# Where the sample's mixer-input splits stand in the ScalarE and DVE queues of a two-request encoder kernel

## The chip, the core and the metric

The kernel runs on one core of one Trainium2 chip. A core has five engines, each with a queue of its own: TensorE (PE, matmuls; PEld are its weight loads), VectorE (DVE), ScalarE (ACT), GpSimd (POOL) and SyncE (SP), which here only issues DMAs. ACT issues the weight loads beside its own work. The metric is the device time of one launch in microseconds (us); lower is better. The time before is 2271.11 us, the median of 3 runs (2269.18 to 2272.93).

## What is computed

One encoder layer is applied to two requests with shared weights: the prompt (1024 positions) and the sample (512 positions), each with 16 learned meta positions in front. Cut to what matters:

```python
n = rms_norm(h)
qa, ka, va, qb, kb, vb = split(n @ w_in)
A = softmax(rope(qa) @ rope(ka).T / 8) @ va          # 8 heads of 64, keys shared by 4
B = (softmax(q0 @ k0.T) - lam * softmax(q1 @ k1.T)) @ vb   # 4 heads, two maps each
h = h + concat(A, B) @ w_out                          # the mixer's output
h = h + conv_glu(rms_norm(h))                         # gate with a width-3 convolution, d_ff 2816
y = rms_norm(h)
```

All of it is float32. To keep that precision on TensorE every matmul operand x is split into two parts, hi = round(x) in the type fp32r and lo = x - hi, and a product is taken as hi*hi + hi*lo + lo*hi.

## The kernel before

Tiles hold features on the 128 partitions and positions along the free axis. The stages follow in the order: projection of the sample, attention of the sample merged with the projection of the prompt, then attention of the prompt (s = 0) merged with the sample's mixer output and ConvGLU (the generator `sample()`), then the prompt's own mixer output and ConvGLU. The change lies at the start of the third of these.

**The merge.** `merge` (L755) takes turns between two generators. With `LEAD2 = 60000` the prompt's attention is written first, for two whole blocks and one softmax of the third; then the sample's work begins. On PE the first four steps of the sample's work are held behind the second block's last matmul (`HOLD`). An attention block is one head with 512 queries: four softmaxes (`softmax`, L394) and one product with the values (`weighted_v`, L411). A softmax is six score matmuls into the one wide PSUM tile `ps_s` (L401, L402), a scaled minimum on DVE that reads it and so frees it (L405), and an exponential on ACT (L408). `weighted_v` transposes the probabilities 128 keys at a time into one of two PSUM tiles `ps_t` (L422), splits them (`split`: the cast `pt_hi` on ACT, L123, and the subtraction `pt_lo` on DVE, L124) and multiplies (L436, L437). The last 32 keys are split into one tile, `pt_hi[0:32]` by ACT and `pt_hi[32:64]` by DVE (L442), and multiplied at L446. `reciprocals` (L450) writes a row of reciprocals to DRAM through a copy on ACT (L457).

**The sample's mixer output.** `mixer_out` (L584) loads the sample's attention output from DRAM into `h` by eight DMAs on SP (L612), one for each 128 features; then come 16 splits, eight feature tiles by two chunks of 258 and 256 positions (L616): the cast `xhi<-h` on ACT and the subtraction `xlo<-h,xhi` on DVE. Then for each of eight tiles of outputs and each chunk come 24 matmuls (`dense`, L134, lines L129 to L131). The residual `res` is loaded by SP (L622), and where the chunk is one position short its last column is set to zero by a small DVE memset (L625).

**What sets the order.** The program goes through a scheduler that simulates a timeline, picks per engine what is ready in that timeline, and fixes one order of instructions for each engine. On the chip every engine goes through its own list in that order; an instruction that waits for a semaphore holds up all that stands behind it on its engine. `tc.issue_after(x)` adds an order: what is traced inside it on the engine of x stands behind x. Memory is taken from pools; a tile that takes the place of an older one waits until the older one's readers are done, DMAs among them. DMAs count on eight semaphores, DMAHW0 to DMAHW7, in turn, and a DMA first waits for the one before it on the same semaphore.

Of the kernel before, what the change touches and what calls it, by code (L numbers as in the profile page):

```python
# [12 lines left out]
F32 = mybir.dt.float32  # L13
F32R = mybir.dt.float32r
AF = mybir.ActivationFunctionType
ALU = mybir.AluOpType
# [6 lines left out]
KT = D // P  # L23
# [39 lines left out]
def token_chunks(s):  # L63


    ends = [c + w + 2 for c, w in even_chunks(SEQS[s], 510)]
    return [(a, b - a) for a, b in zip([0] + ends, ends)]
# [36 lines left out]
def pool(ctx, g, name, bufs, side):  # L104
    return ctx.enter_context(g.tc.tile_pool(name=name, bufs=bufs, side=side, reuse_waits="tile"))
# [14 lines left out]
def split(g, hi, lo, src, lo_engine=None):  # L120

    nc = g.nc
    nc.scalar.copy(hi, src)  # L123
    (lo_engine or nc.vector).tensor_tensor(out=lo, in0=src, in1=hi.bitcast(F32), op=ALU.subtract)  # L124


def mm3(g, ps, whi, wlo, xhi, xlo, start, stop):
# [6 lines left out]
def dense(g, ps, w, xhi, xlo, c0, cw, order=range(KT)):  # L134

    whi, wlo = w
    for i, k in enumerate(order):
        g.mark = mm3(g, ps, whi[:, k * P:(k + 1) * P], wlo[:, k * P:(k + 1) * P],
                     xhi[k][:, c0:c0 + cw], xlo[k][:, c0:c0 + cw], i == 0, i == KT - 1)


def load_weight(g, src, lo_engine=None, hi_engine=None):

    nc = g.nc
    w = g.wp.tile([P, D], F32, name="w_f", tag="w_f", bufs=NRAW)
    nc.scalar.dma_start(out=w, in_=src)
    hi = g.wp.tile([P, D], F32R, name="w_hi", tag="w_hi")
    lo = g.wp.tile([P, D], F32R, name="w_lo", tag="w_lo")
    if hi_engine:
        hi_engine.tensor_copy(hi, w)  # L150
        nc.vector.tensor_tensor(out=lo, in0=w, in1=hi.bitcast(F32), op=ALU.subtract)
    else:
        split(g, hi, lo, w, lo_engine)
    return hi, lo
# [194 lines left out]
def attention(ctx, g, s, side):  # L349
    nc, tc = g.nc, g.tc  # L350
# [14 lines left out]
    op = pool(ctx, g, f"ao{s}", 2, side)  # L365
# [14 lines left out]
    def load_k(j, m):  # L380
        k = kp.tile([P, ne], F32R, name="k", tag="k")
        stacked(k[:, :n], j, m, 0, 0, n)
        if ne > n:
            stacked(k[:, n:], j, m, 0, 0, ne - n)
        return k
# [25 lines left out]
    def weighted_v(pl, v, diff):  # L411

        W = sum(p.shape[0] for p in pl)
        o = g.psum.tile(P, W, "o")
        v, v_tail = v

        def transposed(k0, kw):
            tps = g.psum.tile(kw, W, "t")
            c = 0
            for p in pl:  # L420
                M = p.shape[0]
                nc.tensor.transpose(tps[:, c:c + M], p[:, k0:k0 + kw], g.ident[:M, :M])  # L422
                c += M
            return tps

        for i in range(nf):
            tps = transposed(i * P, P)
            hi = ptp.tile([P, 512], F32R, name="pt_hi", tag="pt_hi")[:, :W]
            lo = ptp.tile([P, 512], F32R, name="pt_lo", tag="pt_lo")[:, :W]
            split(g, hi, lo, tps)  # L430
            if diff:
                nc.tensor.matmul(o, lhsT=v[:, i, 0:P], rhs=hi, start=i == 0, stop=False)  # L432
                nc.tensor.matmul(o, lhsT=v[:, i, P:2 * P], rhs=hi, start=False, stop=False)
                nc.tensor.matmul(o, lhsT=v[:, i, 0:P], rhs=lo, start=False, stop=False)
            else:
                nc.tensor.matmul(o, lhsT=v[:, i, :], rhs=hi, start=i == 0, stop=False)  # L436
                nc.tensor.matmul(o, lhsT=v[:, i, :], rhs=lo, start=False, stop=False)  # L437
            yield 5 * W

        tps = transposed(n - 32, 32)  # L440
        parts = ptp.tile([P, 512], F32R, name="pt_hi", tag="pt_hi")[:, :W]
        split(g, parts[0:32], parts[32:64], tps)  # L442
        if diff:
            nc.scalar.copy(parts[64:96], tps)
        rows = v_tail.shape[0]
        g.mark = nc.tensor.matmul(o, lhsT=v_tail, rhs=parts[:rows], start=False, stop=True).ins  # L446
        yield 2 * W
        return o, W
# [36 lines left out]
    for kv in range(2):  # L485
        k = load_k(KA, kv)
        v = load_v(0, P, kv * P)
        for i in range(4):
            h = kv * 4 + i
            for b in range(nblk):  # L490
                q = load_q(QA + 2 * kv, i, NMETA + 512 * b, 512)
                load_r()
                pl = []
                l = sp.tile([P, 4], F32, name="l_a", tag="l_a", bufs=3)
                for t in range(4):
                    pl.append(softmax([x[:, t * P:(t + 1) * P] for x in q], k, l[:, t:t + 1]))
                    yield 2 * n
                cols = slice(1 + 512 * b, 513 + 512 * b)
                reciprocals(l, g.rT[s][h, cols].rearrange("(t p) -> t p", p=P))
                o, W = yield from weighted_v(pl, v, False)  # L500
                oa = finish_a(o, W)
                store_a()
                late.append((oa, g.rT[s][h:h + 1, cols], g.oT[s][h * HD:(h + 1) * HD, cols]))
# [12 lines left out]
        for i in range(4):  # L516
            h = kv * 4 + i
# [34 lines left out]
    for h in range(4):  # L552
# [3 lines left out]
        for blk in blocks:  # L556
            c0 = blk[0][0]
# [8 lines left out]
def add_square(g, tp, acc, h, j, c0, cw, eng, bufs=2):  # L566

    nc = g.nc
    hs = h[:, j, c0:c0 + cw]
    if j == 0:  # L570
        nc.scalar.activation(acc, hs, AF.Square)
    else:
        sq = tp.tile([P, cw], F32, name="sq", tag="sq", bufs=bufs)
        nc.scalar.activation(sq, hs, AF.Square)
        eng.tensor_tensor(out=acc, in0=acc, in1=sq, op=ALU.add)


def mean_rsqrt(g, tp, out, acc, cw, tag="mm"):
    ps = g.psum.tile(P, cw, tag)
    g.nc.tensor.matmul(ps, lhsT=g.ones_d, rhs=acc, start=True, stop=True)  # L580
    rsqrt_newton(g, tp, out, ps, cw)


def mixer_out(g, s, st, side, whole, tag):  # L584

    nc, tc = g.nc, g.tc
    C = SEQS[s] + 2
    h, rstd = st.h, st.rstd
    chunks = token_chunks(s)
    cm = max(w for _, w in chunks)  # L590
    with ExitStack() as es:
        mp = pool(es, g, f"fm{s}", 3, side)
        waiting = []

        def finish():
            while waiting:
                c0, cw, acc = waiting.pop(0)
                mean_rsqrt(g, mp, rstd[:, c0:c0 + cw], acc, cw, tag)

        for group in ([chunks] if whole else [[c] for c in chunks]):  # L600
            if whole:
                (xhi, xlo), base = [[x[:, k] for k in range(KT)] for x in st.x], 0
            else:
                xhi = [mp.tile([P, cm], F32R, name="xhi", tag=f"xhi{k}", bufs=2) for k in range(KT)]
                xlo = [mp.tile([P, cm], F32R, name="xlo", tag=f"xlo{k}", bufs=2) for k in range(KT)]
                base = group[0][0]
            acc = mp.tile([P, sum(w for _, w in group)], F32, name="acc", tag="acc", bufs=1 if whole else 2)
            if group[0][0] == 0:

                nc.vector.memset(h[:, :, C - 1:], 0.0)  # L610
                for k in range(KT):
                    nc.sync.dma_start(out=h[:, k, :C - 1], in_=g.oT[s][k * P:(k + 1) * P])  # L612
            for k in range(KT):
                for c0, cw in group:
                    b = c0 - base
                    split(g, xhi[k][:, b:b + cw], xlo[k][:, b:b + cw], h[:, k, c0:c0 + cw])  # L616
            for j in range(KT):
                w = load_weight(g, g.w_out[j])
                for c0, cw in group:
                    real = min(cw, C - 1 - c0)  # L620
                    res = mp.tile([P, cm], F32, name="res", tag="res", bufs=4)[:, :cw]
                    nc.sync.dma_start(out=res[:, :real],  # L622
                                      in_=g.xT[s][j * P:(j + 1) * P, NMETA - 1 + c0:NMETA - 1 + c0 + real])
                    if real < cw:
                        nc.vector.memset(res[:, real:], 0.0)  # L625
                    ps = g.psum.tile(P, cw, tag)
                    dense(g, ps, w, xhi, xlo, c0 - base, cw)
                    nc.vector.tensor_tensor(out=h[:, j, c0:c0 + cw], in0=ps, in1=res, op=ALU.add)
                    add_square(g, mp, acc[:, c0 - base:c0 - base + cw], h, j, c0, cw, nc.gpsimd, 1)
                    yield 24 * cw  # L630
                if j == ML:
                    finish()
            waiting += [(c0, cw, acc[:, c0 - base:c0 - base + cw]) for c0, cw in group]
        finish()
# [326 lines left out]
```

## Time and profile before

| | |
|---|---|
| median of 3 runs | 2271.11 us |
| the profiled execution | 2271.76 us |
| its span in the profile | 2270.0 us |
| mean granted TensorE clock | 0.967 |
| PE busy | 2139.6 us (94%) |
| DVE busy | 1272.2 us (56%) |
| ACT busy | 1039.8 us (46%) |
| POOL busy | 669.2 us (29%) |

The profile's times count from the start of its span. A row of the timeline gives start, duration, engine, line of the code, operation, the tile written and the tiles read, shapes, and in brackets how long the engine was idle before the row and what ended that. Rows of SP (SPq) are DMA issues, not the transfers. Tile names in the profile leave the buffer numbers out; in the order of the built program they are kept, so that blocks can be told apart: `pt_hi_6134` to `pt_hi_6222` belong to the prompt's first attention block, `pt_hi_6294` to `pt_hi_6382` to its second, and `p_6399`, `p_6490`, `p_6501`, `p_6512` are the softmaxes of the third; `p_6777` to `p_6842` those of the fourth.

### The profile page before, as it was taken

To read this page: it belongs to the slowest core of one execution; us is meant where nothing else is said; L and a number is where in the kernel's file an instruction comes from. 1 tells how busy PE (TensorE), PEld (TensorE's weight loads), DVE (VectorE), ACT (ScalarE), POOL (GpSimd) and SP (SyncE) were. 2 spreads that over 40 slices of the span, in tenths; PEclk is the share of its full clock that TensorE was granted. 3 is DMA by queue.
4 is the path that set the end of the run, shared out by engine and by line. 5 is a ranking of instruction groups with operands and counts; after the bars stand their busy time and mean duration, and the time that the engine had idled before them with its cause. 6 is when DMAs were issued, how large, how long until landed. Compare 5 with 4: busy or idle time off the path is not lost.

```text
span 2270.0 us, 32333 instructions
## 1 busy us (share of the span) xinstructions
PE 2139.6 (94%) x12442; PEld 1919.7 (85%) x12442; DVE 1272.2 (56%) x2203; ACT 1039.8 (46%) x1830; POOL 669.2 (29%) x514
## 2 busy tenths in 40 slices
PE   7887999986699999999999997999999999999997
PEld 6886999985598888888999996988888888888887
DVE  6635554454558667667777775774433444433446
ACT  5434554656547445466777775542122221122224
POOL 5862345531023212234444443431111001111005
PEclk8998999996899999999999998999999999999999
DMA  6573454443332232233323224631111111111112
GB/s 204 178 221 112 142 162 129 155 157 105 106 102 82 74 101 81 72 94 92 118 94 107 88 69 151 197 99 49 40 47 56 47 47 47 45 40 56 47 38 75
DMA packets 114259, 222.76 MB, mean 98 GB/s; under 512 B 16312, under 2 KB 67384, under 8 KB 113592
## 3 DMA queue, kind: packets, MB, share of 16 engines
q1 hardware_dynamic: 85304, 115.82, 16.0%
q10 hardware_dynamic: 28800, 104.87, 14.8%
q8 instruction: 98, 1.61, 0.3%
q14 instruction: 57, 0.47, 0.1%
HBM read 172.10 MB, written 48.55 MB: 97 GB/s over the span
## 4 chain that ended last, share of the span: by engine, by line
PE 81%; DMA 6%; DVE 5%; ACT 3%; issue 2%; POOL 1%; SPq 1%; DVEq 0%; ACTq 0%; POOLq 0%
PE ps_mm L129 20%; PE ps_mm L130 20%; PE ps_mm L131 20%; PE ps_t L422 5%; PE ps_s L401 3%; PE ps_s L402 3%; PE ps_o L437 2%; PE ps_o L436 1%; DMA q<-qk 1%; DMA v<-v 1%; PE ps_p L129 1%; PE ps_p L131 1%; PE ps_p L130 1%; PE ps_o L432 1%; DMA w_f<-w_out 1%
## 5 line engine op out<-in xcount | busy, mean ns | idle before, releaser
L129 PE MATMUL ps_mm<-xhi,w_hi 128*128 128x512 f32 (+6 forms) x1968 | 666.3, 339 | 0.7 <-ACT xhi L123 0.4
L130 PE MATMUL ps_mm<-xlo,w_hi 128*128 128x512 f32 (+6 forms) x1968 | 659.6, 335 | 0.6 <-POOL xlo L124 0.6
L131 PE MATMUL ps_mm<-xhi,w_lo 128*128 128x512 f32 (+6 forms) x1968 | 658.1, 334 | 0.0
L129 PEld LDWEIGHTS ps_mm<-xhi,w_hi 128*128 128x128 f32 x1968 | 373.7, 190 | 28.1 <-issue 1.7
L130 PEld LDWEIGHTS ps_mm<-xlo,w_hi 128*128 128x128 f32 x1968 | 373.8, 190 | 26.2 <-POOL xlo L124 1.3
L131 PEld LDWEIGHTS ps_mm<-xhi,w_lo 128*128 128x128 f32 x1968 | 373.3, 190 | 25.0 <-issue 0.5
L123 ACT CAST w_hi<-w_f 128x1024 fp32r<-128x1024 f32 x134 | 139.3, 1048 | 402.7 <-PE ps_mm L130 364.2
L405 DVE TENSOR_SCALAR_CACHE_REDUCE p<-ps_s 114x1044 f32<-114x1044 f32 (+5 forms) x212 | 223.4, 1054 | 127.7 <-PE ps_s L402 107.1
L124 POOL TENSOR_TENSOR a_lo<-gate,a_hi 128x512 fp32r<-128x512 f32 x66 | 99.4, 1507 | 660.3 <-ACT a_hi L123 659.3
L123 ACT CAST pt_hi<-ps_t 128x512 fp32r<-128x512 f32 (+6 forms) x360 | 168.9, 482 | 200.3 <-PE ps_t L422 169.7
L703 DVE TENSOR_TENSOR h<-ps_mm,h 128x512 f32<-128x512 f32 (+1 forms) x288 | 182.0, 644 | 121.8 <-PE ps_mm L131 121.1
L408 ACT ACTIVATE p<-p,nm 114x1040 f32<-114x1040 f32 (+5 forms) x212 | 215.2, 1015 | 74.0 <-DVE p L405 73.0
L124 DVE TENSOR_TENSOR pt_lo<-ps_t,pt_hi 128x512 fp32r<-128x512 f32 (+4 forms) x312 | 171.7, 564 | 125.5 <-ACT pt_hi L123 123.7
L130 PE MATMUL ps_mm<-a_lo,w_hi 128*128 128x512 f32 (+1 forms) x576 | 216.1, 378 | 0.0
L131 PE MATMUL ps_mm<-a_hi,w_lo 128*128 128x512 f32 (+1 forms) x576 | 216.1, 378 | 0.0
L129 PE MATMUL ps_mm<-a_hi,w_hi 128*128 128x512 f32 (+1 forms) x576 | 214.8, 385 | 0.4 <-DVE h L703 0.4
L401 PE MATMUL ps_s<-k,q 128*114 128x348 f32 (+4 forms) x552 | 180.8, 333 | 30.8 <-DMA q<-qk 16.9
L422 PE MATMUL ps_t<-ident,p 128*128 128x128 f32 (+7 forms) x1188 | 184.2, 270 | 2.4 <-ACT r_rows L457 2.0
L402 PE MATMUL ps_s<-k,q 128*114 128x348 f32 (+4 forms) x552 | 175.2, 323 | 4.4 <-DMA q<-qk 4.4
L124 DVE TENSOR_TENSOR w_lo<-w_f,w_hi 128x1024 fp32r<-128x1024 f32 x100 | 124.1, 1250 | 82.8 <-ACT w_hi L123 82.7
L422 PEld LDWEIGHTS ps_t<-ident,p 128*128 128x128 f32 (+7 forms) x1188 | 142.9, 136 | 31.7 <-issue 4.0
L532 POOL TENSOR_TENSOR p<-p 114x1040 f32<-114x1040 f32 (+2 forms) x56 | 115.0, 2053 | 128.9 <-ACT p L531 127.0
(189 smaller groups left out, 3547.2 us busy)
## 6 DMA issues: line engine op xcount, KB each, us to landing
w_f<-w_gate ACTq DMA_DIRECT2D x44, 512.0 KB
w_f<-w_up ACTq DMA_DIRECT2D x44, 512.0 KB
w_f<-w_down ACTq DMA_DIRECT2D x44, 512.0 KB
w_f<-w_in ACTq DMA_DIRECT2D x36, 512.0 KB
w_f<-w_out ACTq DMA_DIRECT2D x32, 512.0 KB
q<-qk SPq DMA_DIRECT2D x48, 256.0 KB
q<-qk SPq DMA_DIRECT2D x48, 171.0 KB
qk<-hi SPq DMA_DIRECT2D x20, 384.0 KB
```

The costliest lines, as they stand in the source:

```text
L123: nc.scalar.copy(hi, src)
L124: (lo_engine or nc.vector).tensor_tensor(out=lo, in0=src, in1=hi.bitcast(F32), op=ALU.subtract)
L129: nc.tensor.matmul(ps, lhsT=whi, rhs=xhi, start=start, stop=False)
L130: nc.tensor.matmul(ps, lhsT=whi, rhs=xlo, start=False, stop=False)
L131: return nc.tensor.matmul(ps, lhsT=wlo, rhs=xhi, start=False, stop=stop).ins
L401: nc.tensor.matmul(ps[:, i], lhsT=q[0], rhs=kc, start=True, stop=False)
L402: nc.tensor.matmul(ps[:, i], lhsT=q[1], rhs=kc, start=False, stop=True)
L405: nc.vector.tensor_scalar(out=p.rearrange("p (i w) -> p i w", i=nch), in0=ps, scalar1=-HD ** -0.5, scalar2=3.0e38, op0=ALU.mult, op1=ALU.m ...
L408: nc.scalar.activation(p, p, AF.Exp, bias=nm, scale=-1.0, accum_out=l)
L422: nc.tensor.transpose(tps[:, c:c + M], p[:, k0:k0 + kw], g.ident[:M, :M])
L532: nc.gpsimd.tensor_tensor(out=p0, in0=p0, in1=p1, op=ALU.add)
L703: nc.vector.tensor_tensor(out=hs, in0=ps, in1=hs, op=ALU.add)
```

## The change

`split` returns its two instructions, `weighted_v` keeps those of the last split of its block in `g.marks`, and `mixer_out` for the sample (`whole`) traces its 16 splits inside `issue_after` of both. When `mixer_out` is traced, the marks are those of the prompt's second attention block. So the casts stand behind `pt_hi_6382` on ACT and the subtractions behind `pt_hi_6382` on DVE. No instruction is added or taken away. From the first moved instruction on the scheduler orders anew; the lists of all engines differ up to about PE instruction 7900 of 12323 and are the same behind it.

```diff
 def split(g, hi, lo, src, lo_engine=None):
-    nc.scalar.copy(hi, src)
-    (lo_engine or nc.vector).tensor_tensor(out=lo, in0=src, in1=hi.bitcast(F32), op=ALU.subtract)
+    return (nc.scalar.copy(hi, src),
+            (lo_engine or nc.vector).tensor_tensor(out=lo, in0=src, in1=hi.bitcast(F32), op=ALU.subtract))
...
-        split(g, parts[0:32], parts[32:64], tps)
+        g.marks = [i.ins for i in split(g, parts[0:32], parts[32:64], tps)]
...
-            for k in range(KT):
-                for c0, cw in group:
-                    b = c0 - base
-                    split(g, xhi[k][:, b:b + cw], xlo[k][:, b:b + cw], h[:, k, c0:c0 + cw])
+            with ExitStack() as behind:
+                for mark in g.marks if whole else ():
+                    behind.enter_context(tc.issue_after(mark))
+                for k in range(KT):
+                    for c0, cw in group:
+                        b = c0 - base
+                        split(g, xhi[k][:, b:b + cw], xlo[k][:, b:b + cw], h[:, k, c0:c0 + cw])
```

The order on ACT at the end of the first block, before (line numbers behind L612 are three higher in the changed kernel):

```order
L123 CAST pt_hi_6211<-ps_t_6206 128x512
L123 CAST xhi_6040<-h_6042 128x258
L123 CAST xhi_6040<-h_6042 128x256
L123 CAST pt_hi_6222<-ps_t_6217 32x512
L123 CAST xhi_6040<-h_6042 128x258
L123 CAST xhi_6040<-h_6042 128x256
L123 CAST xhi_6040<-h_6042 128x258
L123 CAST xhi_6040<-h_6042 128x256
L408 ACTIVATE p_6490,l_a_6398<-p_6490,nm_6498 128x1040
```

And on ACT now, at the same place:

```order
L123 CAST pt_hi_6211<-ps_t_6206 128x512
L123 CAST pt_hi_6222<-ps_t_6217 32x512
L408 ACTIVATE p_6490,l_a_6398<-p_6490,nm_6498 128x1040
L457 COPY r_rows_6285<-ps_t_6283 4x128
L462 COPY o_low_6226<-ps_o_6128 64x512
L123 CAST pt_hi_6294<-ps_t_6289 128x512
L408 ACTIVATE p_6501,l_a_6398<-p_6501,nm_6509 128x1040
L123 CAST pt_hi_6305<-ps_t_6300 128x512
```

The 16 casts, which stood between row `pt_hi_6211` and the second block, now follow `pt_hi_6382` in one piece.

The order on DVE at the same place, before; the brackets name the semaphores that a row waits for (DMAHW: DMAs):

```order
L124 TENSOR_TENSOR pt_lo_6212<-ps_t_6206,pt_hi_6211 128x512 [waits Activation_49]
L124 TENSOR_TENSOR xlo_6041<-h_6042,xhi_6040 128x258 [waits DMAHW7_49,DMAHW1_49,Activation_49]
L124 TENSOR_TENSOR xlo_6041<-h_6042,xhi_6040 128x256 [waits Activation_49]
L124 TENSOR_TENSOR pt_hi_6222<-ps_t_6217,pt_hi_6222 32x512 [waits DMAHW5_49,Activation_49]
L625 MEMSET res_6523 128x1 [waits DMAHW2_49,DMAHW0_49]
L124 TENSOR_TENSOR xlo_6041<-h_6042,xhi_6040 128x258 [waits DMAHW2_49,Activation_49]
L124 TENSOR_TENSOR xlo_6041<-h_6042,xhi_6040 128x256 [waits Activation_49]
L124 TENSOR_TENSOR xlo_6041<-h_6042,xhi_6040 128x258 [waits DMAHW3_49,Activation_49]
L405 TENSOR_SCALAR p_6501,nm_6509<-ps_s_6502 128x1044 [waits PE_49]
```

On DVE now:

```order
L124 TENSOR_TENSOR pt_lo_6212<-ps_t_6206,pt_hi_6211 128x512 [waits Activation_49]
L124 TENSOR_TENSOR pt_hi_6222<-ps_t_6217,pt_hi_6222 32x512 [waits DMAHW5_49,Activation_49]
L628 MEMSET res_6523 128x1 [waits DMAHW2_49,DMAHW0_49]
L405 TENSOR_SCALAR p_6501,nm_6509<-ps_s_6502 128x1044 [waits PE_49]
L628 MEMSET res_6653 128x1
L464 TENSOR_TENSOR o_a_6228<-ps_o_6128,o_low_6226 64x512 [waits DMAHW7_49,Activation_49]
L124 TENSOR_TENSOR pt_lo_6295<-ps_t_6289,pt_hi_6294 128x512 [waits Activation_49]
L405 TENSOR_SCALAR p_6512,nm_6520<-ps_s_6513 128x1044 [waits PE_49]
L124 TENSOR_TENSOR pt_lo_6306<-ps_t_6300,pt_hi_6305 128x512 [waits DVE_49,Activation_49]
```

The subtractions have left; the memset of `res_6523` keeps its place behind `pt_hi_6222` and ahead of `p_6501`. By the built program's wait values its DMAHW0 is the count that the store of `o_b_5159` reaches, the last of the sample's attention output, in whose memory `res` lies. The issues on SP there are the same before and now:

```order
L370 DMA q_7104<-qk0_0_60 128x1x512 [waits DMAHW7_49,PE_49]
L563 DMA oT1_88<-o_b_5159 128x306 [waits DMAHW0_49,DVE_49]
L612 DMA h_6042<-oT1_88 128x513 [waits DMAHW1_49]
L612 DMA h_6042<-oT1_88 128x513 [waits DMAHW2_49]
L612 DMA h_6042<-oT1_88 128x513 [waits DMAHW3_49]
L612 DMA h_6042<-oT1_88 128x513
L612 DMA h_6042<-oT1_88 128x513 [waits DMAHW5_49]
L612 DMA h_6042<-oT1_88 128x513 [waits DMAHW6_49]
L612 DMA h_6042<-oT1_88 128x513 [waits DMAHW7_49]
L612 DMA h_6042<-oT1_88 128x513 [waits DMAHW0_49]
```

Here DMAHW6 of the sixth load of `h` is the count of the load of `q_7102`, DMAHW7 of the seventh that of `q_7104`, and DMAHW0 of the eighth again that of the store of `o_b_5159`.

The order on PE behind the second block, before (`ps_mm_6463` and `ps_mm_6526` are the two chunks of the first tile of mixer outputs):

```order
L446 MATMUL ps_o_6288<-pt_hi_6382,v_tail_6070 128x512
L129 MATMUL ps_mm_6463<-xhi_6040,w_hi_6457 128x258
L130 MATMUL ps_mm_6463<-xlo_6041,w_hi_6457 128x258
L131 MATMUL ps_mm_6463<-xhi_6040,w_lo_6458 128x258
L129 MATMUL ps_mm_6463<-xhi_6040,w_hi_6457 128x258
```

On PE now:

```order
L446 MATMUL ps_o_6288<-pt_hi_6382,v_tail_6070 128x512
L129 MATMUL ps_mm_6463<-xhi_6040,w_hi_6457 128x258
L129 MATMUL ps_mm_6526<-xhi_6040,w_hi_6457 128x256
L422 MATMUL ps_t_6561<-ident_93,p_6399 128x128
L422 MATMUL ps_t_6561<-ident_93,p_6490 128x128
L422 MATMUL ps_t_6561<-ident_93,p_6501 128x128
L422 MATMUL ps_t_6561<-ident_93,p_6512 128x128
L130 MATMUL ps_mm_6463<-xlo_6041,w_hi_6457 128x258
L131 MATMUL ps_mm_6463<-xhi_6040,w_lo_6458 128x258
L129 MATMUL ps_mm_6463<-xhi_6040,w_hi_6457 128x258
L130 MATMUL ps_mm_6526<-xlo_6041,w_hi_6457 128x256
```

The 48 matmuls of the two chunks stood one chunk after the other; now they take turns, feature tile by feature tile, with the transposes `ps_t_6561` and `ps_t_6572` and the score matmuls `ps_s_6843` of the attention among them.

## The prediction

> **What bounds the kernel now.** I read the page first, then PE's waits, then the timeline of each engine around the one large wait, and last the busy time by stretches.
>
> ```profile
> span 2270.0 us, 32333 instructions
> PE 2139.6 (94%) x12442; PEld 1919.7 (85%) x12442; DVE 1272.2 (56%) x2203; ACT 1039.8 (46%) x1830; POOL 669.2 (29%) x514
> ...
> PE   7887999986699999999999997999999999999997
> ```
>
> PE is busy 94% of the span. One slice of the 40 is 56.75 us; the dips lie at the start, in slices 10 and 11 (511 to 624 us), in slice 25 and at the end. So an idle gap of PE counts in full, unless later work would have waited anyway. Of PE's waits between 560 and 1400 us one stands out:
>
> ```profile
> PE ps_o L446 <- DVE pt_hi L124: 14.9, 1, 14.9
> ```
>
> The columns are the total, the number of waits and the longest: the 14.9 us are one wait, at the end of the prompt's first attention block. ACT's timeline shows where it comes from:
>
> ```profile
> 578.01 0.58 ACT L123 CAST pt_hi<-ps_t 128x512 fp32r<-128x512 f32 x1 [1.37 <-PE ps_t L422]
> 594.12 0.71 ACT L123 CAST xhi<-h 128x258 fp32r<-128x258 f32 x2 [15.52 <-DMA h<-oT]
> 594.74 0.57 ACT L123 CAST pt_hi<-ps_t 32x512 fp32r<-32x512 f32 x1
> 595.21 1.32 ACT L123 CAST xhi<-h 128x258 fp32r<-128x258 f32 x4
> ```
>
> ACT stood 15.52 us in front of the first cast of `h`, whose load landed at 594.1. Behind it waited `pt_hi_6222` (594.74), behind that DVE's half of it, and behind that PE's L446. DVE and PE in the same stretch:
>
> ```profile
> 597.09 1.23 DVE L405 TENSOR_SCALAR_CACHE_REDUCE p<-ps_s 128x1044 f32<-128x1044 f32 x1
> ...
> 598.59 2.10 DVE L124 TENSOR_TENSOR xlo<-h,xhi 128x258 fp32r<-128x258 f32 x6
> ...
> 603.18 0.69 DVE L124 TENSOR_TENSOR pt_lo<-ps_t,pt_hi 128x512 fp32r<-128x512 f32 x1
> 603.78 1.09 DVE L124 TENSOR_TENSOR xlo<-h,xhi 128x256 fp32r<-128x256 f32 x3
> ```
>
> ```profile
> 596.09 0.79 PE L446 MATMUL ps_o<-pt_hi,v_tail 64*128 64x512 f32 x1 [14.85 <-DVE pt_hi L124]
> ...
> 599.12 1.12 PE L422 MATMUL ps_t<-ident,p 128*128 128x128 f32 x4 [1.19 <-ACT r_rows L457]
> 599.88 0.64 PE L401 MATMUL ps_s<-k,q 128*128 128x348 f32 x1
> ...
> 601.77 0.63 PE L436 MATMUL ps_o<-pt_hi,v 128*128 128x512 f32 x1
> ...
> 615.29 0.41 PE L401 MATMUL ps_s<-k,q 128*128 128x348 f32 x1
> ...
> 616.43 0.49 PE L446 MATMUL ps_o<-pt_hi,v_tail 64*128 64x512 f32 x1
> 616.86 0.39 PE L129 MATMUL ps_mm<-xhi,w_hi 128*128 128x258 f32 x1
> ...
> 622.69 0.40 PE L436 MATMUL ps_o<-pt_hi,v 128*128 128x512 f32 x1
> ```
>
> The second block runs from 596 to 616.9, and the first 48 matmuls of the mixer output from 616.86 to 622.69. From there on the slices show PE full, with windows further down for 680 to 740.
>
> **The change, step by step.** (1) *The 16 casts leave ACT's place in front of `pt_hi_6222`.* The wait for `h` goes there: ACT can cast `pt_hi_6222` at about 578.6 and DVE follows at about 580.2. If nothing else waited, the hole would go as a whole.
>
> (2) *What is late next.* By the order, DVE then goes on to the memset of `res_6523`, which waits for the store of `o_b_5159`, and behind it stands L405 of `p_6501`. That L405 frees the only `ps_s` tile, and PE's next score matmuls (`ps_s_6513`) need it. When does the store land? SP's issues show it:
>
> ```profile
> 582.20 0.49 SPq L474 DMA_DIRECT2D o_rb<-rT  x1
> 582.79 1.13 SPq L370 DMA_DIRECT2D q<-qk  x2
> 584.01 0.43 SPq L563 DMA_DIRECT2D oT<-o_b  x1
> ```
>
> ```profile
> 589.29 0.32 SPq L612 DMA_DIRECT2D h<-oT  x1
> ```
>
> ```profile
> 593.27 0.32 SPq L612 DMA_DIRECT2D h<-oT  x1
> ```
>
> ```profile
> 593.64 0.43 SPq L612 DMA_DIRECT2D h<-oT  x1
> ```
>
> The store is issued at 584.01. The sixth load of `h` (589.29) had waited for `q_7102`, the seventh (593.27) for `q_7104`, and the eighth (593.64) for the store; it went 0.05 us after the seventh was issued, so the store had landed by 593.6, when exactly isn't seen. Bounds: it cannot land before 584.0; the nearest rows are the two DMAs issued just ahead of it, landed at 589.3 and 593.3. I take **593.6**, since `q_7104`, the neighbour in the queue, took until 593.27 and the first `h` load, the neighbour behind, until 594.1. SP's issues up to there don't move, so that time stays.
>
> So the wait for `h` on ACT is exchanged for a wait for a store on DVE that ends only half a microsecond sooner. DVE's memset then starts at 593.6, L405 of `p_6501` at 593.65 and ends at 594.9 (1.23 us), and `ps_s_6513` starts at 594.95. Before it started at 599.88, since DVE's L405 came at 597.09 behind five subtractions, and PE's transposes had waited for ACT's copy `r_rows` behind ten casts. **Gain 4.9 us.** (That copy now waits only for its own buffer, until 582.2, the time at which SP's `o_rb` was released by the same store.)
>
> (3) *From `ps_s_6513` to the block's last matmul* it took 616.43 - 599.88 = 16.55 us. In that chain lay three subtractions of `h` (the row 603.78, 1.0 us without the overlap at its end) and one `pt_lo` (603.18 to 603.78, 0.6 us), which now is done while `ps_s_6513` runs. **Gain 1.6 us.** L446 of the second block comes at 609.9.
>
> Against this stands the clock:
>
> ```profile
> 581.00:596.00 15.00, 0.23 (x2) 0.00 (x0) 1.41 (x3) 1.88 (x6) 0.00 (x0) 0.64 0.65 180
> 596.00:603.30 7.30, 5.12 (x16) 3.70 (x16) 6.87 (x20) 7.25 (x20) 1.39 (x1) 0.57 0.34 108
> 603.30:616.90 13.60, 12.59 (x68) 9.12 (x68) 9.65 (x18) 8.81 (x16) 0.00 (x0) 1.00 0.19 58
> ```
>
> The third number from the end is the granted clock: after the hole it is 0.57 for 7.3 us, then 1.00. With step 2 PE still idles from about 583 to 594.95, so I keep a cold stretch of the same length, and it costs what it costs now; if it reaches one score group further, six matmuls in 1.9 us (599.88 to 601.77) in place of 1.1 (615.29 to 616.43), that is 0.8 us lost, and if it ends sooner, as much won. The Trainium skill, "TensorE: Matmul & The Clock Gate", section "HAM oscillation — how this bites in real kernels", has the rule that a gap of more than about 3.4 us lets the clock fall to half. It agrees with the rows here, and by it the remaining gap is still long enough; only a wait that shrank below that would keep the clock up, which is part of the second rival.
>
> (4) *The splits at their new place.* The 16 casts (0.33 us each by the row of four, 5.3 us) start behind `pt_hi_6382`, at about 607, long after `h` has landed, and hide beside DVE and PE. The 16 subtractions (0.35 us each by the row of six, 5.6 us, and one L405 of 1.23 us among them) run from 609.4 to 616.3, and the 48 matmuls, 5.83 us before, have now among them two groups of transposes and one of scores, 1.7 us that PE did elsewhere before. From 610.3 PE needs 7.5 us, to 617.8; the subtractions end ahead of it. So I cost the pacing at **nothing**, hidden by those groups; without that cover PE would stand for up to the 1.23 us of the L405. Bounds: 0 and +1.3 us.
>
> (5) *Everything behind* is ordered anew up to about 900 us. PE is full from 622 to 680; then come the stretches where the sample's norm is formed:
>
> ```profile
> 680.00:700.00 20.00, 19.15 (x130) 16.91 (x129) 15.10 (x26) 14.39 (x30) 3.63 (x5) 1.00 0.36 105
> 700.00:720.00 20.00, 18.74 (x119) 15.85 (x119) 18.92 (x37) 16.04 (x34) 8.56 (x12) 1.00 0.15 47
> 720.00:740.00 20.00, 19.70 (x137) 17.39 (x137) 16.00 (x30) 13.25 (x27) 7.42 (x9) 1.00 0.29 94
> ```
>
> PE idles 0.85 + 1.26 + 0.30 = 2.4 us there. The new order could save all of it or double it: bounds -2.4 and +2.4 us, taken at 0.
>
> **Sum.** -4.9 - 1.6 = -6.5 us against the profiled execution's own 2271.76 us (span 2270.0 and 1.76 around it): 2265.3 us. That execution stands 0.65 us above the median 2271.11; from the median the sum gives 2264.6. I forecast **2265 us**.
>
> **Rivals.** *A, the forecast:* the hole moves from ACT to DVE and shrinks. For it speaks the memset's place in the order and SP's rows; against it only that the landing of the store is bounded from above and not seen. With the bounds of steps 3 to 5 it gives 2262.5 to 2268.
>
> *B, the store lands much sooner than 593.6.* If it lands with `q_7102`, at 589.3, everything comes 4.3 us sooner still: 2261. If it lands before DVE gets to the memset, the change does all it aims at: 14.85 us of hole, the 1.19 us behind it, 2.2 us of cold clock (5.12 busy us at 0.57 would be 2.9 at full speed) and 1.6 us of step 3 make 20: 2252 us. Against it speaks that its neighbours on both sides landed at 593.3 and 594.1. The Trainium skill, "DMA: Bandwidth & Descriptors", section "Queues, rings and completion order", says that completions aren't in order of issue on one engine's queue. No row here shows the store by itself, so I leave B a real chance.
>
> *C, the gain is given back* within what a measurement can tell: steps 4 and 5 at their bad ends (1.3 and 2.4 us) leave 2.8 us, 2269; with a group of cold matmuls (0.8) 2 us, 2270.
>
> *D, slower:* the new order up to 900 us makes PE wait in the norm stage at 680 to 740. There the sample's chain (L580, L112 to L117, L650, the splits) is covered by attention work, and the new order has drawn attention work forward, away from this cover. PE idles 2.4 us there; from 2.4 + 6.5 = 8.9 us on the gain is gone, and from 13.4 us on the kernel is 4.5 us slower, 2276. Against it: the stretch of 60 us is 96% full.
>
> That the change doesn't move what it says is ruled out by the order.
>
> **How the numbers follow.** 0.2% is 4.5 us, about what a measurement of this kernel can tell from no change: faster means below 2266.6, slower above 2275.6. A 0.60 (0.54 of it faster, 0.06 within), B 0.15 (faster), C 0.19 (within), D 0.06. So faster 0.69, same 0.25, slower 0.06. The range 2256 to 2269.5 leaves out D, the lower part of B (0.06) and the far end of C (0.07).
>
> **What would show it.** In the changed profile ACT has no wait for `h<-oT`; DVE has one row, the memset L628, with some 12.5 us idle ahead of it, ended by a DMA `oT<-o_b`, or the L405 behind it has; PE waits once for about 11.5 us, now in front of L401 and not of L446, at about 583. If the memset's wait is short, B holds; if PE's hole is as said and the time is still above 2268, the loss must show as PE idle time between 617 and 760. If the cold stretch is gone, step 3 is mis-sized. The forecast would be wrong at its root if the hole stayed at L446.

## The result, and the profile after

The changed kernel takes 2266.47 us (median of 20 runs, 2263.56 to 2271.6); the kernel before took 2270.75 us beside it (20 runs, 2266.41 to 2275.03). The medians lie 4.3 us apart, which is 0.19%. The ratio of the compared runs is 0.9984 with a 95% interval of 0.9978 to 0.9990; by it the gain is 3.6 us, between 2.3 and 5.0. The runs can tell this gain from none, but it is just under the 0.2% that the prediction set for "faster". The forecast time was 2265 us.

The page of the changed kernel, its span, the busy times and PE's 40 slices:

```profile
span 2263.0 us, 32334 instructions
...
PE 2135.7 (94%) x12442; PEld 1916.2 (85%) x12442; DVE 1272.5 (56%) x2203; ACT 1040.5 (46%) x1830; POOL 666.2 (29%) x514
...
PE   6887999986799999999999997989999999999997
```

The dip in slices 10 and 11 is smaller and still there. The profiled execution before had a span of 2270.0; 7.0 us between two single executions is more than the medians differ, so the stretches are compared below from one fixed matmul to another. PE's waits from 560 to 1400 us again have one large one (total, number, longest):

```profile
PE ps_s L401 <- DVE res L628: 11.1, 1, 11.1
```

The 14.9 us at L446 are gone, and 11.1 us stand in front of L401. DVE's timeline in this stretch, with the two rows on both sides of its pause:

```profile
579.57 0.68 DVE L124 TENSOR_TENSOR pt_hi<-ps_t,pt_hi 32x512 fp32r<-32x512 f32 x1
591.84 1.24 DVE L405 TENSOR_SCALAR_CACHE_REDUCE p<-ps_s 128x1044 f32<-128x1044 f32 x1 [11.59 <-issue]
591.86 0.06 DVE L628 MEMSET res<- 128x1 f32 x1
```

The memset and the L405 behind it begin together, 11.59 us after the first block's last split. The bracket names no releaser ("issue"): the wait belongs to the memset in the queue ahead of L405, and the profile puts the idle time down to the row that started first. That it is the store has to come from the experiments. SP's issues show when the store went out:

```profile
571.47 0.47 SPq L458 DMA_DIRECT2D rT<-r_rows  x1
579.70 0.49 SPq L474 DMA_DIRECT2D o_rb<-rT  x1
...
581.52 0.43 SPq L563 DMA_DIRECT2D oT<-o_b  x1
582.00 10.42 SPq L612 DMA_DIRECT2D h<-oT  x8
```

SP stood 8.2 us behind the store of `rT`, whose landing `o_rb` needs, and the store of `o_b` stood behind that. From its issue to DVE's start are 10.3 us, in which the eight loads of `h` went out too. PE's and ACT's timelines:

```profile
580.48 0.50 PE L446 MATMUL ps_o<-pt_hi,v_tail 64*128 64x512 f32 x1
...
593.14 0.66 PE L401 MATMUL ps_s<-k,q 128*128 128x348 f32 x1 [11.13 <-DVE res L628]
...
608.39 0.49 PE L446 MATMUL ps_o<-pt_hi,v_tail 64*128 64x512 f32 x1
608.81 0.51 PE L129 MATMUL ps_mm<-xhi,w_hi 128*128 128x258 f32 x2
```

```profile
606.58 5.02 ACT L123 CAST xhi<-h 128x258 fp32r<-128x258 f32 x16
```

The first block's L446 runs without a wait, and the casts of `h` (L123) have no bracket: `h` had long landed when they started.

### The profile page after: what moved, and what is told of

The parts are those of the page before. It is cut to its first block, busy times and chain, and to the rows that moved or that the text cites. A ratio compares the mean times of both kernels' runs of the same rounds, so it can differ in the third digit from the quotient of the medians.

```text
span 2263.0 us, 32334 instructions
## 1 busy us (share of the span) xinstructions
PE 2135.7 (94%) x12442; PEld 1916.2 (85%) x12442; DVE 1272.5 (56%) x2203; ACT 1040.5 (46%) x1830; POOL 666.2 (29%) x514
## 3 DMA queue, kind: packets, MB, share of 16 engines
q10 hardware_dynamic: 28800, 104.87, 14.9%
q8 instruction: 98, 1.61, 0.3%
## 4 chain that ended last, share of the span: by engine, by line
PE 82%; DVE 6%; DMA 5%; issue 3%; ACT 2%; POOL 1%; SPq 0%; DVEq 0%; ACTq 0%; POOLq 0%
PE ps_mm L129 20%; PE ps_mm L130 20%; PE ps_mm L131 20%; PE ps_t L422 5%; PE ps_s L401 4%; PE ps_s L402 3%; PE ps_o L437 2%; PE ps_o L436 2%; DMA q<-qk 1%; PE ps_p L129 1%; PE ps_p L131 1%; PE ps_p L130 1%; DVE p L405 1%; DMA w_f<-w_out 1%; PE ps_o L432 1%
## 5 line engine op out<-in xcount | busy, mean ns | idle before, releaser
L129 PE MATMUL ps_mm<-xhi,w_hi 128*128 128x512 f32 (+6 forms) x1968 | 664.8, 338 | 0.0
L130 PE MATMUL ps_mm<-xlo,w_hi 128*128 128x512 f32 (+6 forms) x1968 | 659.0, 335 | 0.0
L131 PE MATMUL ps_mm<-xhi,w_lo 128*128 128x512 f32 (+6 forms) x1968 | 658.6, 335 | 0.0
L129 PEld LDWEIGHTS ps_mm<-xhi,w_hi 128*128 128x128 f32 x1968 | 373.2, 190 | 26.7 <-issue 1.0
L130 PEld LDWEIGHTS ps_mm<-xlo,w_hi 128*128 128x128 f32 x1968 | 373.3, 190 | 25.0 <-issue 0.7
L131 PEld LDWEIGHTS ps_mm<-xhi,w_lo 128*128 128x128 f32 x1968 | 373.0, 190 | 24.7 <-issue 0.2
L123 ACT CAST w_hi<-w_f 128x1024 fp32r<-128x1024 f32 x134 | 139.5, 1049 | 398.6 <-PE ps_mm L130 359.9
L405 DVE TENSOR_SCALAR_CACHE_REDUCE p<-ps_s 114x1044 f32<-114x1044 f32 (+5 forms) x212 | 223.6, 1055 | 140.9 <-PE ps_s L402 110.8
L123 ACT CAST pt_hi<-ps_t 128x512 fp32r<-128x512 f32 (+6 forms) x360 | 169.2, 483 | 203.3 <-PE ps_t L422 173.2
L401 PE MATMUL ps_s<-k,q 128*114 128x348 f32 (+4 forms) x552 | 181.9, 335 | 41.1 <-DMA q<-qk 16.4
L130 PE MATMUL ps_mm<-a_lo,w_hi 128*128 128x512 f32 (+1 forms) x576 | 216.4, 379 | 0.0
L131 PE MATMUL ps_mm<-a_hi,w_lo 128*128 128x512 f32 (+1 forms) x576 | 216.1, 378 | 0.0
L129 PE MATMUL ps_mm<-a_hi,w_hi 128*128 128x512 f32 (+1 forms) x576 | 215.1, 385 | 0.4 <-DVE h L706 0.4
L422 PE MATMUL ps_t<-ident,p 128*128 128x128 f32 (+7 forms) x1188 | 183.8, 270 | 0.4 <-DVE pt_lo L124 0.3
L402 PE MATMUL ps_s<-k,q 128*114 128x348 f32 (+4 forms) x552 | 175.8, 324 | 4.3 <-DMA q<-qk 4.3
L422 PEld LDWEIGHTS ps_t<-ident,p 128*128 128x128 f32 (+7 forms) x1188 | 142.9, 136 | 29.1 <-issue 4.5
```

What stands on the lines that cost most here:

```text
L123: return (nc.scalar.copy(hi, src), (lo_engine or nc.vector).tensor_tensor(out=lo, in0=src, in1=hi.bitcast(F32), op=ALU.subtract))
L129: nc.tensor.matmul(ps, lhsT=whi, rhs=xhi, start=start, stop=False)
L130: nc.tensor.matmul(ps, lhsT=whi, rhs=xlo, start=False, stop=False)
L131: return nc.tensor.matmul(ps, lhsT=wlo, rhs=xhi, start=False, stop=stop).ins
L401: nc.tensor.matmul(ps[:, i], lhsT=q[0], rhs=kc, start=True, stop=False)
L402: nc.tensor.matmul(ps[:, i], lhsT=q[1], rhs=kc, start=False, stop=True)
```

## The experiments

Each was timed in five rounds beside the kernel before; the medians of the latter were 2269.64 (e1 to e4), 2268.61 (e5 to e8) and 2269.41 us (e9 to e11).

### e1: the store that the memset waits for

```diff
-            nc.sync.dma_start(out=rows[:, c1:c1 + W - lead], in_=ob[:, lead:])
+            (nc.gpsimd if s == 1 and h == 3 and blk is blocks[-1] else nc.sync).dma_start(out=rows[:, c1:c1 + W - lead], in_=ob[:, lead:])
```

> The changed kernel, but the sample attention's last store of o_b (L563) is issued by GpSimd instead of SyncE; PE's and ACT's order stay as they are. Theory (the hole now hangs on this store: DVE's memset L628 waits for its landing, L405 behind it, PE's L401 behind that): the store goes out at about 574, lands by about 580, the memset waits for nothing, the 11.1 us wait of PE in front of L401 goes and 2 us of halved clock with it; 13 us less than the changed kernel, 2252 to 2256. Rival 1 (another transfer or engine holds the memset or L405 until 592, the store only seemed to): 2265 to 2268, the wait of about 11 us stays. Rival 2 (work behind the block gives the gain back): the 11 us wait is gone, the time is above 2260 and PE idles later.

2251.46 us, ratio 0.9921 (0.9907 to 0.9934). Of its profile: POOL's issue of the store, DVE's memset and L405, and PE's largest wait in the stretch:

```profile
574.86 0.74 POOL L563 DMA_DIRECT2D oT<-o_b  x1 [21.79 <-DVE o_b L544]
```

```profile
581.32 1.24 DVE L405 TENSOR_SCALAR_CACHE_REDUCE p<-ps_s 128x1044 f32<-128x1044 f32 x1
581.34 0.06 DVE L628 MEMSET res<- 128x1 f32 x1
```

```profile
583.91 0.66 PE L422 MATMUL ps_t<-ident,p 128*128 128x128 f32 x4 [1.31 <-ACT r_rows L457]
584.33 0.41 PE L401 MATMUL ps_s<-k,q 128*128 128x348 f32 x1
...
597.82 0.50 PE L446 MATMUL ps_o<-pt_hi,v_tail 64*128 64x512 f32 x1
```

The memset waits for nothing, L401 starts 2.8 us after the first block's end, and the time falls as the theory said, to half a microsecond below its range. Rivals 1 and 2 are out: the store was what held DVE, and no new wait of that size takes the place. From L401 to the second block's L446 it takes 13.49 us here (597.82 - 584.33) and 15.25 in the changed kernel (608.39 - 593.14), with the same matmuls in the same order and waits of the same length among them: the halved clock after the hole costs 1.8 us.

### e2: the same store, without the change

The edit of e1 in the kernel before.

> The kernel before, with the same store on GpSimd; the casts stay where they were. Theory (two waits end half a microsecond apart, that for the load of h on ACT covers that for the store): PE's wait of 14.9 us at L446 stays, since h lands as late as before; 0 to 1.5 us less than before, 2269 to 2271. Rival (the store alone is the cause, and the casts needn't move): 2254 to 2262.

2267.82 us, ratio 0.9997 (0.9987 to 1.0007): no change. The expectation named the wrong place: the scheduler now put `pt_hi_6222` ahead of the casts, so L446 is free, and the wait stands a few matmuls further on. PE's waits and ACT's timeline:

```profile
PE ps_t L422 <- ACT r_rows L457: 16.8, 3, 15.8
```

```profile
590.82 1.32 ACT L123 CAST xhi<-h 128x258 fp32r<-128x258 f32 x4 [14.86 <-DMA h<-oT]
```

ACT still stands 14.86 us in front of the casts. So the early store brings nothing without the move of the casts, and with it some 14 us (the ratio of e1 against that of the changed kernel, 0.9921 against 0.9984): the two waits lay side by side, and each covered the other.

### e3: the casts behind the first block

The marks are those of the block before the last one, so the splits stand right behind `pt_hi_6222`.

```diff
-        g.marks = [i.ins for i in split(g, parts[0:32], parts[32:64], tps)]
+        g.older, g.marks = getattr(g, 'marks', []), [i.ins for i in split(g, parts[0:32], parts[32:64], tps)]
...
-                for mark in g.marks if whole else ():
+                for mark in g.older if whole else ():
```

> The changed kernel, but the marks are those of the prompt's first attention block, so the casts stand right behind the cast of pt_hi_6222 and no longer behind the second block. PE's order then differs from that of before in 116 rows only. Theory (PE has only 2 to 3 us of work behind L446 until it needs DVE's L405, which stands behind two subtractions and so behind the load of h): the wait moves from L446 to L401 with about 12 to 13 us, s_6513 starts at 597 to 600; 2268 to 2271. Rival (freeing L446 is what brings the gain, and the rest of the change is nothing): 2265 to 2267.5.

2269.9 us, ratio 1.0001 (0.9992 to 1.0011). L446 is freed as in the change; PE's waits and DVE's row:

```profile
PE ps_s L401 <- DVE p L405: 16.2, 6, 14.1
```

```profile
592.72 0.77 DVE L124 TENSOR_TENSOR xlo<-h,xhi 128x258 fp32r<-128x258 f32 x2 [12.60 <-ACT xhi L123]
```

The hole is in front of L401 with 14.1 us, since L405 stands behind subtractions that wait for `h`. Freeing L446 by itself is worth nothing; PE has under 2 us of work before it needs L405.

### e4: the store on ACT

As e1, with `nc.scalar` in place of `nc.gpsimd`.

> The changed kernel, but the same store is issued by ACT, where it stands behind L408 of the first block's scores; PE's order and ACT's are otherwise the same. Theory: as with GpSimd, the store goes out at about 574 to 575, lands by about 581, the 11 us wait of PE goes; 2252 to 2257, with at most 1 us lost to the issue on ACT. If the store is late here too, because the transfers of q and h share its time rather than because of its place on SyncE, the wait shrinks only by the 7 us of earlier issue: 2259 to 2262.

2254.02 us, ratio 0.9933 (0.9921 to 0.9945). The hole is gone here too, but the price of the issue, at most 1 us in the theory, was put too low. ACT's and PE's timelines:

```profile
577.67 0.34 ACTq L563 DMA_DIRECT2D oT<-o_b  x1
578.11 1.07 ACT L123 CAST pt_hi<-ps_t 128x512 fp32r<-128x512 f32 x2 [2.64 <-DMA k<-qk]
```

```profile
578.74 0.50 PE L436 MATMUL ps_o<-pt_hi,v 128*128 128x512 f32 x1 [1.61 <-ACT pt_hi L123]
```

By the bracket ACT first waits 2.6 us for an earlier DMA (`k`), issues the store, and only then goes on to its casts; PE waits 1.6 us for them.

### e9 and e5: the memset on GpSimd

The other end of the same wait. e9 is the changed kernel with this edit alone, e5 has the edit of e1 as well.

```diff
-                        nc.vector.memset(res[:, real:], 0.0)
+                        nc.gpsimd.memset(res[:, real:], 0.0)
```

> As e1_store_pool (the changed kernel with the store on GpSimd), and the memsets of res (L628) on GpSimd too. That leaves the place of the hole as it is in e1 (no wait of 11 us), but the order of all engines behind the second block is another one (6933 rows of PE's). Theory (the changed kernel and e1 lose 1.6 us between 740 and 860 because of the order of PE's instructions there, without a wait that shows): the stretch from the prompt block's last L446 at about 564 to the one at about 958 takes anything from 375 to 379 us, since the order is new, and not just 377.0. Rival (what is lost there is the price of being early, the same for every kernel without the hole): 377.0 within 0.3 us again. Time: 2249 to 2254.

> The changed kernel with only the memsets of res (L628) on GpSimd; the store stays on SyncE and lands at about 592 as before. The order of all engines behind the second block is nearly that of e5_memset_pool. Theory (what held PE was DVE standing at the memset, not the store as such): GpSimd now waits for the store, DVE goes on to L405 at about 580, PE's wait of 11 us at L401 is gone; the time is within 3 us of e5's 2243.7, 2242 to 2248. Rival (the late store also holds something else that PE needs, the release of a tile or SyncE's loads): the wait stays in another place, 2254 or more.

e5 took 2243.7 us, ratio 0.9894 (0.9881 to 0.9906); e9 2243.18 us, ratio 0.9884 (0.9868 to 0.9901). Of e9, POOL and DVE:

```profile
592.48 0.13 POOL L628 MEMSET res<- 128x1 f32 x2 [40.43 <-DMA oT<-o_b]
```

```profile
580.33 1.25 DVE L405 TENSOR_SCALAR_CACHE_REDUCE p<-ps_s 128x1044 f32<-128x1044 f32 x1
```

This settles step 2 from the other side: the store still lands at 592 (now the bracket names it), POOL stands and waits, nobody needs POOL, DVE goes on at 580.33, and PE's longest wait between 560 and 700 us is 0.7 us. Both are 8 us below e1, more than the hole explains and below the range expected of e5. The whole order behind is another one in these two (the change of the memset's engine changes the scheduler's timeline), and this order is better; which part of it brings the 8 us was not followed up, so these two runs show where the hole hung and not what the memset's place is worth by itself. The question that e5 was to settle on the stretch from 564 to 958 stays open: in the new order that stretch holds 2294 matmuls in place of 2329, so its 369.1 us can't be set beside the 377.0 of e1.

e10 is the kernel before with this edit alone.

> The kernel before with only the memsets of res on GpSimd; the splits stay where they were and PE's order is the same as before. Theory: ACT's wait for h still holds the first block's last cast, the memset was never late there; PE waits 14 to 16 us as before, 2268 to 2271. Rival (the memsets on DVE were the hindrance all along): 2260 or less.

2269.97 us, ratio 1.0001 (0.9992 to 1.0010), PE's wait at L446 14.7 us: as with e2, neither edit is worth anything without the other.

### e6, e7, e8: the loads of h on GpSimd

e6 is the kernel before, e7 is e3, e8 is e1; in each the store and the eight loads of `h` are issued by GpSimd.

```diff
-                    nc.sync.dma_start(out=h[:, k, :C - 1], in_=g.oT[s][k * P:(k + 1) * P])
+                    (nc.gpsimd if whole else nc.sync).dma_start(out=h[:, k, :C - 1], in_=g.oT[s][k * P:(k + 1) * P])
```

> The kernel before, with the store (L563) and the eight loads of h (L612) on GpSimd; the splits are not moved by a mark. Theory (the first hole is the load of h, issued late because SyncE stands 8 us on the store of rT in front of it): the loads go out at 576 to 582, the first lands at about 582, the last at about 590; casts stand on ACT ahead of the second block's work, so PE still waits, but in pieces: 3 to 8 us instead of 14.9; 2257 to 2263. Rival (what costs is the 16 casts and subtractions in the second block's way, not the load): 2266 to 2270.

> The changed kernel with the marks of the prompt's first block (as e3_behind_first), the store and the loads of h on GpSimd. Theory: like e6, since the casts stand in nearly the same place: 2256 to 2263, and 6 to 13 us less than e3. Rival (a late h is not what held e3): 2267 to 2271.

> As e1_store_pool, with the eight loads of h on GpSimd too; the order of PE and ACT is that of e1. Theory (with the splits behind the second block, h has landed by 596 when the first cast stands ready, so its load is covered wholly): within 1.5 us of e1, 2250 to 2253. Rival (SyncE, freed of the loads, brings the loads behind them earlier, and these were late): 2247 or less.

e6 took 2257.58 us, ratio 0.9954 (0.9942 to 0.9966), e7 2258.54 us, 0.9957 (0.9945 to 0.9969). In e6 the scheduler put `pt_hi_6222` ahead of the casts, as in e2, so e6 is to be read against e2 (0.9997), and e7 against e3 (1.0001): some 10 us less each. The first hole hung on `h` being late, and an early load opens most of it with the casts still in front of the second block's work. e8 took 2257.04 us, 0.9945 (0.9932 to 0.9957): 5.6 us more than e1, where both theories saw none or a gain. Its profile shows two waits. The first is the old one, on DVE:

```profile
581.08 0.09 DVE L628 MEMSET res<- 128x1 f32 x2 [3.83 <-DMA oT<-o_b]
```

The order on DVE is another one here: the memset stands one L405 earlier than in e1, where that L405 ran at 578.71 and the memset came behind it. So it stands at the store again although the store is early, and PE waits 3.4 us in front of L401. (e6 and e7 have the same with 2.7 and 2.9 us on DVE.) For the second wait, SP and POOL first, then ACT:

```profile
573.86 0.45 SPq L458 DMA_DIRECT2D rT<-r_rows  x1
588.80 0.49 SPq L474 DMA_DIRECT2D o_rb<-rT  x1
```

```profile
575.18 3.78 POOL L612 DMA_DIRECT2D h<-oT  x7
```

```profile
588.87 0.26 ACT L457 COPY r_rows<-ps_t 4x128 f32<-4x128 f32 x1 [5.20 <-DMA rT<-r_rows]
```

The loads of `h` (256.5 KB each) now go out between 575 and 579, just behind the store of `rT`. That store, 2 KB, lets `o_rb` go after 14.9 us, against 8.8 in e1 (574.75 to 583.54). The single buffer of `r_rows` is free only then, ACT stands 5.2 us, and PE waits 3.0 us behind it. So `h` being early is no use when the splits wait for the second block anyway, and the small store that it delays is on PE's path. How the 5.6 us divide between the memset's new place and the late `o_rb` was not measured.

### e11: how far the difference varies

The changed kernel itself again.

> The changed kernel itself once more, to see how far its difference varies between comparisons. The first comparison gave 4.3 us less than before, the traces 5.4 us within the stages that changed. Theory: 3 to 6 us less, 2264 to 2267 beside a kernel before at 2269 to 2271.

2266.0 us, ratio 0.9983 (0.9975 to 0.9992): 3.4 us less by the medians, 3.9 by the ratio, between 1.8 and 5.7. PE's wait in front of L401 is 11.2 us.

## Where the gain went, from fixed matmul to fixed matmul

The L446 with 96x306 operands at about 564 us (the sample's last) and a certain L446 of the prompt near 950 have the same 2329 matmuls between them in before, in the changed kernel and in e1 to e4. A third L446 in between splits the stretch. The windows between them, of before, the changed kernel, e1 and e3 (length, busy us and count of PE, PEld, DVE, ACT, POOL, then clock, DMA share, GB/s):

```profile
564.17:646.87 82.70, 63.34 (x406) 53.73 (x406) 45.63 (x89) 42.20 (x85) 7.29 (x7) 0.90 0.36 105
646.87:958.25 311.38, 308.97 (x1925) 270.71 (x1924) 219.63 (x361) 164.57 (x297) 76.14 (x72) 1.00 0.28 84
```

```profile
563.51:638.90 75.39, 61.84 (x401) 53.97 (x401) 45.90 (x91) 42.76 (x87) 6.89 (x6) 0.91 0.38 113
638.90:952.14 313.24, 310.93 (x1930) 271.47 (x1929) 218.91 (x360) 163.98 (x296) 73.05 (x72) 1.00 0.28 84
```

```profile
564.53:628.34 63.81, 60.03 (x400) 51.85 (x401) 45.85 (x91) 42.60 (x87) 8.94 (x7) 1.00 0.46 135
628.34:941.56 313.22, 310.93 (x1931) 271.44 (x1930) 218.90 (x360) 163.80 (x296) 73.22 (x72) 1.00 0.28 84
```

```profile
563.38:645.40 82.02, 64.86 (x405) 55.17 (x405) 45.70 (x89) 42.27 (x85) 7.30 (x7) 0.88 0.35 105
645.40:956.83 311.43, 309.01 (x1926) 270.74 (x1925) 219.73 (x361) 164.66 (x297) 76.27 (x72) 1.00 0.27 84
```

In the first window the change gains 82.70 - 75.39 = 7.3 us. Five matmuls fewer lie in it, work that it has to make up later. Which ones, the groups of this window by line and form show, two of before and the same two of the changed kernel (count, then busy us and mean ns):

```profile
L401 PE MATMUL ps_s<-k,q 128*128 128x348 f32 x30 | 11.0, 368 | 2.3 <-DVE p L405 2.2
L129 PE MATMUL ps_mm<-xhi,w_hi 128*128 128x256 f32 x29 | 8.3, 287 | 0.0
```

```profile
L401 PE MATMUL ps_s<-k,q 128*128 128x348 f32 x33 | 12.2, 372 | 12.7 <-DVE res L628 11.1 <-DVE p L405 1.5
L129 PE MATMUL ps_mm<-xhi,w_hi 128*128 128x256 f32 x25 | 7.2, 288 | 0.0
```

L402 changes as L401 does, L130 and L131 as L129, and one small transpose (L455) is added: the changed kernel has done 12 matmuls of the mixer output less here, and six score matmuls and the transpose more. Matmuls overlap, so what one costs is its distance to the next, in the timeline 0.12 us for the former, 0.16 for a score and about 0.1 for the transpose. That makes 12 * 0.12 - 6 * 0.16 - 0.1 = 0.4 us of work that has only moved, and **6.9 us** of real gain. In the second window the change takes 313.24 - 311.38 = 1.86 us more, 0.4 for the moved work and **1.5 us lost**. Over both it is 394.08 - 388.63 = 5.45 us; the execution of e11 gives 388.64 by the same two matmuls.

The loss stands in every kernel with the changed kernel's order behind the block (313.24, and 313.22 to 313.25 in e1, e4, e8 and e11, in e1 10 us earlier), and in none with the order of before (311.38, and 311.34 to 311.43 in e2, e3 and e10). So it goes with the order of PE's instructions and not with being early. PE idles no more than before there (313.24 - 310.93 = 2.31 us against 2.41), so the loss is in the busy time and not in waiting; what makes it was not resolved.

Behind these windows the changed kernel's order is the same as before, and the profiled executions of before, the changed kernel and e1 to e4 differ there without a pattern: from the last of the three matmuls to the end of the span they take 1307.5 to 1312.6 us. That is why two spans can differ by 7.0 us where the stretch differs by 5.4. The medians differ by 4.3 and 3.4; the stretch lies above the first comparison's interval (up to 5.0) and inside the second's (up to 5.7), and where the rest goes is not shown.

## Why the prediction was right, and what it mis-sized

The time came within its range and the mechanism was the forecast one, rival A. By its steps:

**(1) The casts leave the place in front of `pt_hi_6222`.** Right: no cast waits for `h`, and L446 is at 580.48 without a wait.

**(2) The hole goes to DVE's memset behind the store.** Right in mechanism, and shown from both ends: an earlier store (e1, e4) and a memset on another engine (e9) each take the hole away, and neither does so without the moved casts (e2, e10). The size was 4.9 us; counted from the L446 near 564, `ps_s_6513` comes 35.71 us later before (599.88 - 564.17) and 29.63 after (593.14 - 563.51), so 6.1. What differed is the landing: 593.6 was taken, 29.4 us behind that L446, and it was 591.84, 28.3 us behind it. "SP's issues up to there don't move" holds for their order, not for their times: the store was issued 18.0 us behind that L446, not 19.8 (584.01 - 564.17). The issue of `o_rb`, on which this hangs, lies 18.0 us behind that L446 before and 17.8 in e10, but 16.2 in the changed kernel and 16.4 in its second execution (e11), and 17.5 to 19.0 in e1 to e4. The step had no bounds for this. Whether it is a spread between executions or belongs to the changed kernel is not shown.

**(3) The rest of the second block.** From `ps_s_6513` to L446 it took 15.25 us against 16.55, a gain of 1.3 where 1.6 was forecast. That the subtractions brought it is not shown by itself: four transposes, which before stood in this chain (L422 at 614.88), now run behind L446 (at 609.15). The clock stayed low as assumed; the windows of the changed kernel:

```profile
593.10:598.30 5.20, 5.16 (x17) 4.76 (x18) 3.68 (x6) 2.98 (x5) 1.27 (x1) 0.51 0.69 237
598.30:608.40 10.10, 9.11 (x54) 7.01 (x53) 7.18 (x14) 6.76 (x16) 0.00 (x0) 1.00 0.24 77
```

0.51 for 5.2 us, against 0.57 for 7.3; e1, without a long gap, shows that it costs 1.8 us. The rule drawn on in this step, a gap of more than about 3.4 us halves the clock (the Trainium skill, "TensorE: Matmul & The Clock Gate", section "HAM oscillation — how this bites in real kernels"), fits the 11.13 us here; its figure does not fit shorter gaps (last section).

**(4) The splits at their new place cost nothing.** Right: from L446 of the second block to 616.4, the end of the first 48 matmuls of the mixer output, PE has no idle time.

```profile
608.40:616.40 8.00, 8.00 (x64) 7.76 (x64) 8.00 (x21) 7.95 (x20) 0.00 (x1) 1.00 0.07 27
```

**(5) Everything behind, ordered anew, at 0 with bounds of 2.4 us either way.** This term was mis-sized: it is 1.5 us of loss, within its bounds and of the sign of rival C. The bounds were built on PE's idle time at 680 to 740; the loss is in the busy time.

**Sum.** Steps 1 to 4 were forecast at 6.5 us, and 6.9 were found at the end of the third block: 6.1 and 1.3 from steps 2 and 3, less 0.4 of work that only moved and 0.1 lost on the way. Step 5 gave 1.5 back, and 5.4 are left. So the mechanism was right, and that the time came within 1.5 us of the forecast is in part luck: step 2 was put 1.2 us too small, step 3 too large by 0.3, and step 5 at nothing. The sign was missed by little. "Faster" was the likeliest, at 0.69 and with a bound of 4.5 us, and the medians of the two comparisons say 4.3 and 3.4, which is "same" by that bound.

Rival B, by which the store might land early, came to 1 us in this kernel; but its price for the whole hole, 20 us, was near: e1 takes 18.2 us less than the kernel before beside it, the loss of step 5 included. Rivals C and D looked for the loss in idle time; C had its sign right.

## What to carry to other kernels

When a wait is taken away, look for the next wait in the queue of every engine behind it before counting the gain: here ACT's wait for `h` and DVE's wait for a store covered each other, and taking away the one or the other alone was worth little or nothing. A trivial instruction with a memory dependence, such as a one-column memset into a recycled tile, can hold a whole engine; here it was better put on one for which nobody waits. That one line, on top of the change, brought it from 2266 to 2243 us, of which some 8 us came with a new order that the edit set off and that nobody chose. Compare two profiles between matmuls that enclose the same work, not by their spans.

## What was not expected of the hardware

**A small store can wait for large loads.** From the issue of `rT`'s store (2 KB) to the issue of `o_rb`, which waits for its landing, it takes 8.2 to 8.8 us in the ten traces in which the loads of `h` (2.1 MB) go out later, and 13.3 to 14.9 in e6, e7 and e8, in which they go out in between. The store of `o_b` (153 KB) behaves otherwise. Issued by GpSimd it landed after 5.2 us in e1, while the DMA engines were 34% busy, and after 5.5 us in e8, where seven loads of `h` were issued right behind it and they were 83% busy. (The memset behind it went on 6.7 us after the issue in e8.) The rows are from the lists of DMA issues of e1 and e8 (KB each, median us to landing):

```profile
oT<-o_b POOLq DMA_DIRECT2D x1, 153.0 KB, 5.2
```

```profile
oT<-o_b POOLq DMA_DIRECT2D x1, 153.0 KB, 5.5
```

Issued by SP it took 9.5 us in e9 (583.00 to POOL's row at 592.48) and about 10.3 in the changed kernel. The loads of `h` by themselves don't explain that; whether it is the engine that issues or the transfers of `q` just ahead in SP's queue was not separated.

**Short gaps are enough for the clock.** In e6 the stretch in which PE's longest gap is 2.28 us is followed by 10 us at half clock, in which a second gap of 2.73 us lies:

```profile
579.52 0.43 PE L401 MATMUL ps_s<-k,q 128*128 128x348 f32 x1 [2.28 <-DVE p L405]
```

```profile
577.20:580.50 3.30, 1.02 (x7) 0.98 (x7) 2.31 (x6) 1.14 (x4) 0.55 (x2) 1.00 1.03 328
580.50:590.50 10.00, 7.27 (x26) 5.45 (x25) 6.26 (x14) 5.98 (x16) 1.27 (x1) 0.50 0.48 148
```

In e4 a gap of 1.61 us (its row is above) is followed by a granted clock of 0.56 from 579.5 to 583.4; the 1.31 us in e1 left the clock at 1.00. Behind these short gaps (and 2.53 us in e7) the slow matmuls begin only 0.4 to 1 us after PE has started again, and so the fall looks like a slow stretch that nobody caused.
